# First norm taken for four tiles together, its sums and scalings split between ScalarE and VectorE; x loaded first, the root's table first, first weights in order of use

## The chip, the cores and the metric

One NeuronCore of one Trainium2 chip runs the whole program in one launch. The metric is device time in microseconds (us), as the median of several runs. The engines are named as the profile names them: PE is TensorE (PEld its weight loads), DVE is VectorE, ACT is ScalarE, POOL is GpSimd, SP is SyncE, whose queue issues nearly all DMAs here.

## The reference, cut to what matters

Two transformer blocks follow each other on x of 1024 tokens by 1024 features in float32. The change is in the first lines of the first block:

```python
def rmsnorm(x, w):
    y = x * lax.rsqrt(jnp.mean(x * x, axis=-1, keepdims=True) + EPS)
    return y * w

mem_n = rmsnorm(mem, norm_mem_w)                      # mem: 256 x 1024
proj = rmsnorm(h, norm_mix_w) @ w_in                  # h = x
ca, cb, rq, rk, rv, rg = jnp.split(proj, cuts, axis=-1)
u = ca * jax.nn.sigmoid(cb)                           # 512 channels each
y = depthwise_conv_31(u) + conv_b                     # causal, 31 taps
```

Behind them come a retention over rq, rk, rv and rg, a cross attention to mem_n, a feed-forward layer, and the second block with windowed attention and 16 experts. None of these is edited.

## The kernel before, in words

x is handled as eight tiles of 128 rows (tokens) by 1024 features, in two halves of four tiles, and mem as two such tiles. For each tile `unit_rows` sums the squares on ACT (`sumsq`, L182), takes the root of the mean (`rsqrt_of`, L164 to L175: one small instruction on ACT, L166, and six on DVE) and scales the tile on DVE (L189). `to_fm` then transposes the four tiles of a half on PE (L222, each 128x128 block by itself into `ptT`), and writes for each of the eight feature blocks a pair `hT`: a rounded high part on ACT (L204), and on DVE the rest (L205). Every product is made of three matmuls (L139, L140, L141) from such pairs. A weight unit of 512 KB is loaded as `raw` (three buffers) and split into a pair `w` (five buffers) by ACT (L114) and DVE (L115).

The first products are `cb` and `ca`, 24 matmuls each for a block of 128 channels and a half of the tokens; `sg` is the sigmoid of `cb` (L381) and `uh` the product with `ca` (L385). Each `u` goes to DRAM and comes back for the convolution, 31 DVE instructions for each of four channel blocks (L393, L395). Their result `y` also goes to DRAM and comes back as `yh`, which PE transposes into `yc` (L565). The convolution stands in the program with a low priority, so that its instructions fill DVE beside the next products (`qk`, `v`, `rg`), and beside the retention, which goes through eight tiles in turn (`qkT`, `qbd`, `sc`, `pf`, `yin`, `yT`, `kv`). `km` is the key product of the cross attention; it does not depend on the retention, and stands between its matmuls.

Each engine and the SP queue work strictly in their own order. A scheduler sets that order from priorities and from its own estimates; `tc.high_priority(offset=...)` moves what is written under it ahead by so many places.

Of the kernel before, what the change touches and what calls it, by code (L numbers as in the profile page):

```python
# [12 lines left out]
BF = mybir.dt.bfloat16  # L13
I32 = mybir.dt.int32
U32 = mybir.dt.uint32
AF = mybir.ActivationFunctionType
OP = mybir.AluOpType
# [4 lines left out]
D = 1024  # L22
# [12 lines left out]
def tile_kernel(ctx: ExitStack, tc: tile.TileContext, d, out, stop=None, dbg=None):  # L35
    nc = tc.nc
    pe, act, dve, pool = nc.tensor, nc.scalar, nc.vector, nc.gpsimd
# [21 lines left out]
    def R(i, shape, dt=F32, name="r"):  # L59
        return sb.tile(shape, dt, tag=f"R{i}", bufs=1, name=nm(name))  # L60
# [22 lines left out]


    ident = cst.tile([128, 128], F32, name="ident")
    with tc.high_priority(offset=4500):
        nc.sync.dma_start(ident, d["ident"])
    small = cst.tile([128, 216], F32, name="small")
    with tc.high_priority(offset=4000):
        nc.sync.dma_start(small, d["small"])  # L90
    kc = cst.tile([128, 40], F32, name="kc")
    nc.sync.dma_start(kc, d["kconst"])
# [33 lines left out]
    def wunits(src, i0, n, ahead=1500):  # L126

        res = []
        with tc.high_priority(offset=ahead):
            for u in range(i0, i0 + n):  # L130
                raw = raw_unit(src[u])
                w = sb.tile([128, 2, 1024], F32R, tag=f"W{w_ring[0]()}", bufs=1, name=nm("w"))
                split(w[:, 0, :], w[:, 1, :], raw)
                res.append(w)
        return res
# [52 lines left out]
    def unit_rows(x):  # L188
        dve.tensor_scalar(x, x, row_rstd(x), None, op0=OP.mult)  # L189
        return x  # L190

    def scaled(dst, x, r, gain):
        dve.scalar_tensor_tensor(dst, x, r, gain, op0=OP.mult, op1=OP.mult)
# [22 lines left out]
    def to_fm(xs, regs, banks, name="hT", gain=None, shift=None):  # L216

        res = []
        for k, reg in enumerate(regs):
            p = B(banks(), "ptT")  # L220
            for j, x in enumerate(xs):
                pe.transpose(p[:, j * 128:(j + 1) * 128], x[:, k * 128:(k + 1) * 128], ident)  # L222
            h = R(reg, [128, 2, 512], F32R, name=name)
            evac_split(h[:, 0, :], h[:, 1, :], p, col(gain, k), col(shift, k))
            res.append(h)
        return res
# [66 lines left out]
    def rows(t, n=1):  # L293
        return slice(t * 128, (t + n) * 128)
# [5 lines left out]
    def load(t, src):  # L300
        nc.sync.dma_start(t, src)
        return t
# [13 lines left out]
    pm = Ring([0, 1, 2, 3, 4])  # L316
    pt = Ring([5, 6, 7])
    hT = {}
    for half in range(2):
        with tc.high_priority(offset=4000 if half == 0 else 0):  # L320
            xs = [load(R([17, 18, 19, 20, 24, 25, 26, 27][half * 4 + j], [128, 1024], name="x"), x_d[rows(half * 4 + j), :])
                  for j in range(4)]
            hT[half] = to_fm([unit_rows(x) for x in xs], H[half], pt, gain=g_in)

    xs = [unit_rows(load(R(28 + j, [128, 1024], name="mem"), d["mem"][rows(j), :])) for j in range(2)]
    memT = fm_pairs(xs, [16, 22, 23, 32], pt, g_mem)


# [43 lines left out]
    tr = Ring([0, 1])  # L372
    tr2 = Ring([2, 3])
    for c in range(4):
        ua, ub = wunits(d["w_in_fm"], 2 * c, 2)
        for half in range(2):
            sl = slice(half * HALF, (half + 1) * HALF)
            p = B(pm(), "cb")
            fm_block(p, ub, half_of(hT, half))
            sg = T(tr(), [128, 512], name="sg")  # L380
            act.activation(sg, p, AF.Sigmoid)  # L381
            p = B(pm(), "ca")
            fm_block(p, ua, half_of(hT, half))
            uh = T(tr2(), [128, 512], name="uh")
            dve.tensor_mul(uh, p, sg)  # L385
            store(u_d[c][:, sl], uh)
# [422 lines left out]
    for t in range(8):  # L809
        x = acc[t]  # L810
# [480 lines left out]
def layout(inputs):  # L1291
    f = {k: np.asarray(v) for k, v in inputs.items()}
    a = dict(_constants())
    a["x"] = f["x"][0]
    a["positions"] = np.ascontiguousarray(f["positions"].reshape(8, 128).T)
    small = np.zeros((128, 216), np.float32)
    small[:, 0:124] = np.transpose(f["conv_w"].reshape(31, 4, 128), (2, 1, 0)).reshape(128, 124)
    small[:, 124:128] = _colp(f["conv_b"])
    small[:, 128:140] = np.transpose(f["conv_w_2"].reshape(3, 4, 128), (2, 1, 0)).reshape(128, 12)
    for i, n in enumerate(("norm_mix_w", "norm_xattn_w", "norm_mlp_w", "norm_mem_w")):  # L1300
        small[:, 156 + 8 * i:164 + 8 * i] = _colp(f[n])
    small[:, 188:196] = _colp(f["g_mix_2"][0])
    small[:, 196:204] = _colp(f["g_ffn_2"][0])
    for i, n in enumerate(("ret_gn_w", "conv_ln_w", "conv_ln_b")):
        small[:, 204 + 4 * i:208 + 4 * i] = _colp(f[n])
    a["small"] = small
    a["norm_f_w"] = f["norm_f_w"]
    a["g_ffn"] = f["g_ffn_2"][0]
    a["g_final"] = f["g_final_2"]
    a["sink"] = f["sink_2"][0]  # L1310
    a["mem"] = f["mem"][0]
    a["ctx"] = f["ctx_2"][0]
    bcol = _colp(f["b_ada_2"][0])
    a["b_col"] = np.ascontiguousarray(np.concatenate([bcol, bcol[:, :16]], 1))
    a["c_rows"] = np.stack([f["c_2"][0], f["c_ctx_2"]])
    W = f["w_in"]
    a["w_in_fm"] = _fm(W, [x for c in range(4) for x in (c * 128, 512 + c * 128)])
    a["w_in_tm"] = _tm(W, [2048, 1024, 1536])
    a["w_out_tm"] = _tm(f["w_out"], [0, 512])
    a["xk_fm"] = _fm(f["xkv_w"], range(0, 1024, 128))  # L1320
    a["xv_tm"] = _tm(f["xkv_w"], [1024, 1536])
    a["xq_fm"] = _fm(f["xq_w"], range(0, 1024, 128))
    a["xo_tm"] = _tm(f["xo_w"], [0, 512])
    a["up_fm"] = _fm(f["mlp_up_w"], range(0, 4096, 128))
    dn = f["mlp_down_w"]
    chunks, r0 = [], 0
    for fbs in MLP_CHUNKS:
        chunks.append(_tm(dn[r0:r0 + fbs * 128], [0, 512]))
        r0 += fbs * 128
    a["down_tm"] = np.concatenate(chunks, 0)  # L1330
    a["w_ada"] = np.ascontiguousarray(f["w_ada_2"][0].T.reshape(48, 128, 1024))
    W = f["w_in_2"][0]
    a["w_in2_q"] = _tm(W, [0])
    b = W[:, 512:768].reshape(2, 4, 128, 256)
    a["w_in2_kv"] = np.ascontiguousarray(np.transpose(b, (0, 2, 1, 3)).reshape(2, 128, 1024))
    a["w_in2_fm"] = _fm(W, [x for c in range(4) for x in (1280 + c * 128, 1792 + c * 128, 768 + c * 128)])
    a["w_out2_tm"] = _tm(f["w_out_2"][0], [0, 512])
    a["w_router"] = np.ascontiguousarray(np.transpose(f["w_router_2"][0].reshape(8, 128, 16), (1, 0, 2)).reshape(128, 128))
    wg, wu, wd = f["w_gate_2"][0], f["w_up_2"][0], f["w_down_2"][0]
    ex = []  # L1340
    for e in range(16):
        for nb in (0, 512):
            ex += [_tm(wg[e], [nb]), _tm(wu[e], [nb])]
        for kp in (0, 512):
            ex += [_tm(wd[e][kp:kp + 512], [0, 512])]
    a["experts"] = np.concatenate(ex, 0)
    return a
# [19 lines left out]
```

## Time and profile before

| | |
|---|---|
| median of 3 runs | 2571.12 us (2568.53 to 2572.6) |
| the profiled execution | 2569.4 us, its span 2567.6 us |
| PE busy | 2433.2 us, 95% of the span |
| DVE busy | 1792.5 us, 70% |
| ACT busy | 1164.9 us, 45% |
| granted TensorE clock, mean | 0.98 |

The span is the time from the first to the last instruction; the rest of the execution's own time lies around it. Busy shares are means over stages that differ: in some PE is the only full engine, in some DVE is full too.

### The profile page before, as it was taken

What the parts mean: (1) busy time and instruction counts of PE and PEld (TensorE: products, weight loads), DVE (VectorE), ACT (ScalarE), POOL (GpSimd) and SP (SyncE); (2) the same over time, 40 slices, a digit from 0 to 9 for tenths busy, and PEclk for the clock granted to TensorE, in tenths of its full rate; (3) what the DMA queues carried; (4) which work ended last, traced back from release to release, by engine and by line L of the source; (5) the groups of instructions that cost most, each with busy time, mean ns of one, the idle gap of its engine ahead of it and who ended that gap; (6) DMA issues with size and microseconds to landing.
All of it is one profiled execution on the core that took longest, in us unless ns stands there. A gap on an engine that the chain in (4) does not pass through costs nothing.

```text
span 2567.6 us, 31478 instructions
## 1 busy us (share of the span) xinstructions
PE 2433.2 (95%) x11473; PEld 1971.9 (77%) x11473; DVE 1792.5 (70%) x3204; ACT 1164.9 (45%) x1783; POOL 54.5 (2%) x35
## 2 busy tenths in 40 slices
PE   7999899999999999999999999998973999999996
PEld 5887678888878888888888777776863888888774
DVE  6999783655577555333336858876567999999888
ACT  6113552544442122112214635554332888887775
POOL 0000000000000000000000000000000110101100
PEclk9999999999999999999999999999986999999998
DMA  5233545425443344211112221125673999999993
GB/s 192 87 122 119 161 160 193 142 97 164 137 155 123 119 144 156 64 42 48 58 50 78 92 74 50 42 62 171 219 272 112 384 397 390 390 391 385 354 349 148
DMA packets 138476, 442.34 MB, mean 172 GB/s; under 512 B 15664, under 2 KB 20304, under 8 KB 138320
## 3 DMA queue, kind: packets, MB, share of 16 engines
q1 hardware_dynamic: 133856, 424.07, 46.4%
q0 software_dynamic: 4464, 16.25, 2.6%
q8 instruction: 90, 1.47, 0.2%
q14 instruction: 66, 0.54, 0.1%
HBM read 388.34 MB, written 51.92 MB: 171 GB/s over the span
## 4 chain that ended last, share of the span: by engine, by line
PE 82%; DVE 8%; DMA 5%; ACT 3%; issue 2%; SPq 0%; ACTq 0%; DVEq 0%; POOLq 0%
PE up L140 7%; PE up L141 7%; PE up L139 7%; PE dn L140 6%; PE dn L141 6%; PE dn L139 6%; PE wo L139 3%; PE wo L140 3%; PE wo L141 3%; PE ga L140 2%; PE ga L141 2%; PE ga L139 2%; DVE w L115 2%; PE q L140 2%; PE q L141 2%
## 5 line engine op out<-in xcount | busy, mean ns | idle before, releaser
L114 ACT ACTIVATE w<-raw 128x1024 fp32r<-128x1024 f32 x560 | 584.3, 1059 | 752.1 <-PE dn L141 266.4
L115 DVE TENSOR_TENSOR w<-raw,w 128x1024 fp32r<-128x1024 f32 x560 | 673.5, 1222 | 187.7 <-ACT w L114 180.8
L139 PE MATMUL dn<-w,uT 128*128 128x512 f32 x512 | 199.4, 390 | 1.8 <-ACT relu L754 1.6
L139 PE MATMUL up<-hm,w 128*128 128x512 f32 x512 | 199.6, 390 | 0.0
L140 PE MATMUL up<-hm,w 128*128 128x512 f32 x512 | 199.4, 389 | 0.0
L141 PE MATMUL up<-hm,w 128*128 128x512 f32 x512 | 199.3, 389 | 0.0
L140 PE MATMUL dn<-w,uT 128*128 128x512 f32 x512 | 199.0, 389 | 0.0
L141 PE MATMUL dn<-w,uT 128*128 128x512 f32 x512 | 198.6, 389 | 0.0
L773 DVE TENSOR_TENSOR acc<-dn,acc 128x512 f32<-128x512 f32 x144 | 97.9, 687 | 91.8 <-PE dn L141 91.4
L738 DVE CUSTOM_DVE_ANT_0 mws<-wada,crow 128x512 bf16<-128x512 f32 x128 | 88.2, 689 | 103.0 <-DMA wada<-w_ada 101.0
L395 DVE SCALAR_TENSOR_TENSOR y<-u,small,y 128x1007 f32<-128x1007 f32 (+26 forms) x120 | 146.2, 1260 | 0.5
L139 PEld LDWEIGHTS dn<-w,uT 128*128 128x128 f32 x512 | 96.1, 188 | 22.9 <-ACT relu L754 2.3
L141 PEld LDWEIGHTS up<-hm,w 128*128 128x128 f32 x512 | 96.1, 188 | 20.0
L141 PEld LDWEIGHTS dn<-w,uT 128*128 128x128 f32 x512 | 96.0, 188 | 20.1 <-DVE uT L759 0.2
L139 PEld LDWEIGHTS up<-hm,w 128*128 128x128 f32 x512 | 96.0, 188 | 20.0 <-ACT hm L204 0.3
L140 PEld LDWEIGHTS dn<-w,uT 128*128 128x128 f32 x512 | 96.1, 188 | 19.8
L140 PEld LDWEIGHTS up<-hm,w 128*128 128x128 f32 x512 | 96.1, 188 | 19.8
L140 PE MATMUL ga<-w,x1T 128*128 128x512 f32 x256 | 102.5, 400 | 1.7 <-DVE w L115 1.7
L140 PE MATMUL dn<-w,x1T 128*128 128x512 f32 x256 | 101.6, 397 | 2.0 <-DVE w L115 2.0
L139 PE MATMUL dn<-w,x1T 128*128 128x512 f32 x256 | 102.3, 400 | 0.0
L141 PE MATMUL ga<-w,x1T 128*128 128x512 f32 x256 | 102.0, 398 | 0.0
L140 PE MATMUL up<-w,x1T 128*128 128x512 f32 x256 | 101.6, 397 | 0.0
(414 smaller groups left out, 5471.2 us busy)
## 6 DMA issues: line engine op xcount, KB each, us to landing
raw<-experts SPq DMA_DIRECT2D x384, 512.0 KB, 7.2
wada<-w_ada SPq DMA_DIRECT2D x48, 512.0 KB, 3.5
raw<-up_fm SPq DMA_DIRECT2D x32, 512.0 KB, 3.6
raw<-down_tm SPq DMA_DIRECT2D x32, 512.0 KB, 3.6
raw<-w_out_tm SPq DMA_DIRECT2D x24, 512.0 KB, 3.9
raw<-w_in_fm SPq DMA_DIRECT2D x20, 512.0 KB, 3.8
h_d<-hx SPq DMA_DIRECT2D x32, 256.0 KB, 2.4
raw<-xq_fm SPq DMA_DIRECT2D x16, 512.0 KB, 4.3
```

Of the source, the lines that this page charges most:

```text
L114: act.activation(hi, src, AF.Copy)
L115: dve.tensor_sub(lo, src, hi.bitcast(F32))
L139: pe.matmul(out_, l[0], r[0], start=first, stop=False)
L140: pe.matmul(out_, l[0], r[1], start=False, stop=False)
L141: pe.matmul(out_, l[1], r[0], start=False, stop=last)
L395: dve.scalar_tensor_tensor(yc[:, s:], uc[:, :1024 - s], convw[:, c, 30 - s:31 - s], yc[:, s:], op0=OP.mult, op1=OP.add)
L738: dve.tensor_tensor_reduce(out=mjunk, in0=raw[:, h * 512:(h + 1) * 512], in1=crow[o, h], op0=OP.mult, op1=OP.add, scale=1.0, scalar=0.0, a ...
L773: dve.tensor_add(acc[t][:, sl], p, acc[t][:, sl])
```

## The change

`unit_tiles` takes a list of tiles. It puts the sums of squares of its tiles into the columns of one small tile, those of even tiles on ACT, those of odd tiles on DVE (a new instruction, `tensor_tensor_reduce`); it takes the roots of all columns at once; then it scales even tiles on DVE and odd ones on ACT. It is used for both halves of x and for the two tiles of mem. The loads of the constants `ident` and `small` now stand behind those of x, a root of a constant at the start brings the root's table to ACT, and of each pair of weight units the one for `cb` now comes first.

```diff
-    with tc.high_priority(offset=4500):
+    with tc.high_priority(offset=3900):
         nc.sync.dma_start(ident, d["ident"])
     small = cst.tile([128, 216], F32, name="small")
-    with tc.high_priority(offset=4000):
+    with tc.high_priority(offset=3890):
         nc.sync.dma_start(small, d["small"])
...
+    junk2 = T(6, [128, 1024], BF, name="junk2")
+
+    def unit_tiles(xs):
+
+        n = len(xs)
+        ss = tiny([128, n])
+        for j, x in enumerate(xs):
+            if j % 2 == 0:
+                act.activation(junk, x, AF.Square, accum_out=ss[:, j:j + 1])
+            else:
+                dve.tensor_tensor_reduce(out=junk2, in0=x, in1=x, op0=OP.mult, op1=OP.add, scale=1.0, scalar=0.0,
+                                         accum_out=ss[:, j:j + 1])
+        r = rsqrt_of(ss, 1.0 / D, n)
+        for j, x in enumerate(xs):
+            if j % 2 == 0:
+                dve.tensor_scalar(x, x, r[:, j:j + 1], None, op0=OP.mult)
+            else:
+                act.activation(x, x, AF.Copy, scale=r[:, j:j + 1])
+        return xs
...
+    warm = tiny([128, 1])
+    with tc.high_priority(offset=4500):
+        dve.memset(warm, 1.0)
+        act.activation(warm, warm, AF.Sqrt)
...
-            hT[half] = to_fm([unit_rows(x) for x in xs], H[half], pt, gain=g_in)
-
-    xs = [unit_rows(load(R(28 + j, [128, 1024], name="mem"), d["mem"][rows(j), :])) for j in range(2)]
+            hT[half] = to_fm(unit_tiles(xs), H[half], pt, gain=g_in)
+
+    xs = unit_tiles([load(R(28 + j, [128, 1024], name="mem"), d["mem"][rows(j), :]) for j in range(2)])
...
-        ua, ub = wunits(d["w_in_fm"], 2 * c, 2)
+        ub, ua = wunits(d["w_in_fm"], 2 * c, 2)
...
-    a["w_in_fm"] = _fm(W, [x for c in range(4) for x in (c * 128, 512 + c * 128)])
+    a["w_in_fm"] = _fm(W, [x for c in range(4) for x in (512 + c * 128, c * 128)])
```

The lines behind the edits move by 20 to 24 (L204 becomes L224, L565 becomes L589). The scheduler's order changes in two stretches: in the first 320 matmuls, and again where the retention, `km` and `yc` are mixed. Behind that PE's order is the same as before.

ACT at the program's start, before (`x_73` to `x_79` are the four tiles of the first half):

```order
L182 ACT_TABLE_LOAD
L182 ACTIVATE junk,y_81<-x_73 128x1024
L182 ACTIVATE junk,y_96<-x_75 128x1024
L166 ACT_TABLE_LOAD
L166 ACTIVATE y_85<-y_83 128x1
L182 ACTIVATE junk,y_111<-x_77 128x1024
L166 ACTIVATE y_100<-y_98 128x1
L182 ACTIVATE junk,y_126<-x_79 128x1024
L166 ACTIVATE y_115<-y_113 128x1
L166 ACTIVATE y_130<-y_128 128x1
L114 ACTIVATE w_447<-raw_445 128x1024
L114 ACTIVATE w_452<-raw_450 128x1024
```

The same place now (`x_77` to `x_83` are the four tiles; their even ones are summed here, their odd ones scaled):

```order
L342 ACT_TABLE_LOAD
L342 ACTIVATE y_74<-y_74 128x1
L200 ACTIVATE junk,y_85<-x_77 128x1024
L200 ACTIVATE junk,y_85<-x_81 128x1024
L166 ACTIVATE y_92<-y_90 128x4
L209 ACTIVATE x_79<-x_79,y_100 128x1024
L209 ACTIVATE x_83<-x_83,y_100 128x1024
L114 ACTIVATE w_360<-raw_358 128x1024
L224 ACTIVATE hT_111<-ptT_106,small 128x512
L224 ACTIVATE hT_119<-ptT_114,small 128x512
L224 ACTIVATE hT_127<-ptT_122,small 128x512
```

Four sums, four roots and a table load became two sums, one root and two scalings; one weight split stands between them and the first `hT`, where before there were three.

ACT where the second half is normed, before (`x_205` to `x_211` are its tiles):

```order
L166 ACTIVATE y_217<-y_215 128x1
L182 ACTIVATE junk,y_228<-x_207 128x1024
L381 ACT_TABLE_LOAD
L381 ACTIVATE sg_480<-cb_455 128x512
L166 ACT_TABLE_LOAD
L166 ACTIVATE y_232<-y_230 128x1
L182 ACTIVATE junk,y_243<-x_209 128x1024
L166 ACTIVATE y_247<-y_245 128x1
L182 ACTIVATE junk,y_258<-x_211 128x1024
```

And now (`x_170` to `x_176`; `cb_488` is the second channel block's product, `ws` the angles of the rotary embedding):

```order
L200 ACTIVATE junk,y_267<-mem_263 128x1024
L405 ACTIVATE sg_513<-cb_488 128x512
L166 ACT_TABLE_LOAD
L166 ACTIVATE y_272<-y_270 128x2
L166 ACTIVATE y_185<-y_183 128x4
L209 ACTIVATE mem_265<-mem_265,y_280 128x1024
L209 ACTIVATE x_172<-x_172,y_193 128x1024
L209 ACTIVATE x_176<-x_176,y_193 128x1024
L391 ACT_TABLE_LOAD
L391 ACTIVATE ws_328<-ws_328 128x128
L224 ACTIVATE hT_204<-ptT_199,small 128x512
```

The root of the second half now stands behind a sigmoid that reads the second channel block's product, and its first `hT` behind a table load and a sine. On SP the last tile, `x_176`, is issued behind three weight loads, the last of which waits for the split of the fifth unit; before, the last tile stood behind two.

PE in the retention's fourth tile, before (`kv`, `sc`, `yin`, `yx` are the retention, `km` the filler):

```order
L141 MATMUL km_2944<-hP_406,w_2941 128x256
L453 MATMUL qkT_2127<-ident,qr_2123 128x128 x4
L462 MATMUL sc_2137<-qbd_1396,qkT_1755 128x512
L499 MATMUL kv_2046<-vl_2001,kz_2044 128x256 x2
L462 MATMUL sc_2141<-qbd_1396,qkT_1755 128x512
L471 MATMUL yin_2146<-pf_2139,vl_2125 128x256 x2
L484 MATMUL yx_2162<-St_1395,qkT_1755 128x256
L565 MATMUL yc_2626<-ident,yh_2621 128x128
L565 MATMUL yc_2649<-ident,yh_2621 128x128
```

And now:

```order
L141 MATMUL km_2981<-hP_289,w_2973 128x256
L139 MATMUL km_2981<-hP_299,w_2973 128x256
L523 MATMUL kv_1959<-vl_1914,kz_1957 128x256 x2
L486 MATMUL sc_2050<-qbd_1309,qkT_1668 128x512
L486 MATMUL sc_2054<-qbd_1309,qkT_1668 128x512
L495 MATMUL yin_2059<-pf_2052,vl_2038 128x256 x2
L508 MATMUL yx_2075<-St_1308,qkT_1668 128x256
L589 MATMUL yc_2539<-ident,yh_2534 128x128
L589 MATMUL yc_2562<-ident,yh_2534 128x128
```

`kv` now stands ahead of both `sc`, and seven more `km` ahead of it. Before, the first two `yc` that read the third and fourth channel block stood 22 `km` ahead of this place, among those of the first head; now they stand behind the whole of it.

## Rows read from the trace of the kernel before

**Rows 1.** The page's chain that ended last: shares of the span by engine.

```profile
PE 82%; DVE 8%; DMA 5%; ACT 3%; issue 2%; SPq 0%; ACTq 0%; DVEq 0%; POOLq 0%
```

**Rows 2.** Windows: stretch, its length, busy us of each engine, granted clock, DMA.

```profile
core 0: us, PE busy (x) PEld busy (x) DVE busy (x) ACT busy (x) POOL busy (x), PEclk, DMA share, GB/s
0.00:19.00 19.00, 3.67 (x13) 2.07 (x13) 9.11 (x32) 11.22 (x19) 0.20 (x4) 1.00 0.76 269
5.00:10.00 5.00, 0.00 (x0) 0.00 (x0) 0.52 (x4) 4.06 (x7) 0.00 (x0) 1.00 1.01 411
52.00:225.00 173.00, 173.00 (x764) 143.28 (x764) 164.61 (x166) 30.97 (x39) 0.00 (x0) 1.00 0.33 110
272.00:285.00 13.00, 7.60 (x35) 6.12 (x34) 5.82 (x23) 6.06 (x10) 0.00 (x0) 0.75 0.58 189
285.00:300.50 15.50, 15.24 (x79) 11.98 (x79) 10.86 (x43) 8.48 (x18) 0.00 (x0) 0.88 0.30 92
400.00:2567.00 2167.00, 2062.86 (x9735) 1676.85 (x9733) 1446.70 (x2485) 1003.24 (x1497) 54.30 (x31) 0.98 0.51 178
```

**Rows 3.** Timeline of the first half: start, duration, engine, instruction, [idle before <-releaser].

```profile
1.64 1.85 SPq L301 DMA_DIRECT2D x<-x  x4
5.52 1.06 ACT L182 ACTIVATE junk<-x 128x1024 bf16<-128x1024 f32 x1 [3.50 <-DMA x<-x]
7.06 1.06 ACT L182 ACTIVATE junk<-x 128x1024 bf16<-128x1024 f32 x1 [0.40 <-DMA x<-x]
8.23 1.28 ACT L166 ACT_TABLE_LOAD   x1
9.76 0.16 DVE L168 RECIPROCAL y<-y 128x1 f32<-128x1 f32 x1 [1.36 <-ACT y L166]
10.73 0.75 DVE L189 TENSOR_SCALAR x<-x,y 128x1024 f32<-128x1024 f32 x1
16.89 0.74 DVE L189 TENSOR_SCALAR x<-x,y 128x1024 f32<-128x1024 f32 x1
18.20 1.84 ACT L204 ACTIVATE hT<-ptT,small 128x512 fp32r<-128x512 f32 x3 [2.74 <-PE ptT L222]
18.94 0.80 PE L139 MATMUL cb<-hT,w 128*128 128x512 f32 x1 [0.35 <-ACT hT L204]
28.42 0.39 PE L141 MATMUL cb<-hT,w 128*128 128x512 f32 x1
```

**Rows 4.** Instruction groups by form, 0 to 60 us: count, busy us, mean ns, idle before.

```profile
L205 DVE SCALAR_TENSOR_TENSOR hT<-ptT,small,hT 128x512 fp32r<-128x512 f32 x16 | 11.6, 745 | 1.6 <-ACT hT L204 1.6
L115 DVE TENSOR_TENSOR w<-raw,w 128x1024 fp32r<-128x1024 f32 x7 | 8.6, 1222 | 1.0 <-ACT w L114 1.0
```

**Rows 5.** The page's costliest groups: the only DVE instruction with a sum.

```profile
L738 DVE CUSTOM_DVE_ANT_0 mws<-wada,crow 128x512 bf16<-128x512 f32 x128 | 88.2, 689 | 103.0 <-DMA wada<-w_ada 101.0
```

**Rows 6.** Timeline of the second half's norm and of the first product.

```profile
29.12 0.43 SPq L301 DMA_DIRECT2D x<-x  x1
35.30 1.06 ACT L182 ACTIVATE junk<-x 128x1024 bf16<-128x1024 f32 x1 [1.25 <-DMA x<-x]
39.69 0.74 DVE L189 TENSOR_SCALAR x<-x,y 128x1024 f32<-128x1024 f32 x1
40.84 1.84 ACT L204 ACTIVATE hT<-ptT,small 128x512 fp32r<-128x512 f32 x3 [1.27 <-PE ptT L222]
52.07 0.39 PE L140 MATMUL ca<-hT,w 128*128 128x512 f32 x1
57.58 0.69 DVE L385 TENSOR_TENSOR uh<-ca,sg 128x512 f32<-128x512 f32 x1 [2.07 <-PE ca L141]
```

**Rows 7.** Timeline: start of the convolution, and PE's two longest waits behind it.

```profile
64.68 0.82 DVE L393 TENSOR_SCALAR y<-u,small 128x1024 f32<-128x1024 f32 x1 [0.76 <-DMA u<-u]
274.53 0.44 PE L565 MATMUL yc<-ident,yh 128*128 128x128 f32 x2 [2.09 <-DMA yh<-y]
282.85 2.07 PE L462 MATMUL sc<-qbd,qkT 128*128 128x512 f32 x2 [3.31 <-ACT qbd L458]
```

## The prediction

> **What bounds the kernel now.** The chain that ended last comes first: 82% of it is PE [rows 1]. The windows then show where PE is not full [rows 2]. Until 19 us it is busy for 3.7 us, so over 15 us pass before the first product. From 52 to 225 us it never stops: 764 matmuls in 173 us, 0.226 us each. From 400 us on it is busy for 2062.9 of 2167 us. Those later stages are not edited and their order does not move, so a lead that PE has at 400 us should stand at the end. The place to look for a loss on the way is DVE, which is busy for 164.6 of the same 173 us: the convolution fills it from 64.68 on [rows 7]. From 272 to 285 us both engines have holes, PE 5.4 us and DVE 7.2 us, and PE's granted clock is 0.75 there [rows 2]; its two long waits are named in [rows 7]. So three places decide: the start, the second half's norm near 40 us, and the stretch from 272 us.
>
> **First half.** Four issues of x take 1.85 us, so two fewer ahead of x bring it 0.9 us forward: the first sum, which waits for its tile until 5.52, starts at 4.6. The second tile came 1.54 us behind the first [rows 3]; at the 411 GB/s of that stretch [rows 2] a tile of 0.52 MB takes 1.28. With 1.4, the four land at 4.6, 6.0, 7.4 and 8.8. ACT sums the first and third beside the landing. The last sum is DVE's, an instruction that this trace lacks. Its nearest row sums 512 columns from two sources in 0.69 us [rows 5], and a two-source DVE pass over 1024 takes 1.22 [rows 4]; with reading the sum out I take 1.3. The lower bound is ACT's 1.06 [rows 3], the upper one twice the pass, 2.4. So the sums stand at 10.1. The mean and the root add 0.4, the reciprocal and its polish 0.97 (from 9.76 to 10.73), so scaling starts at 11.5. DVE's two scalings (0.75 each) lie beside ACT's two, 1.06 each: ACT ends at 13.55. Before, the last tile's scaling ended at 16.89 + 0.74 = 17.63. What goes: the second table load (1.28, at 8.23) and a root behind each sum on ACT.
>
> Then ACT's order puts a weight split (a pass over 1024, 1.06) ahead of the first `hT`, which lasts 0.69: PE's first `cb` starts at 15.25, where it started at 18.94, 3.7 us earlier. The eight rests of `hT` on DVE (0.745 each) pace the block, with three weight splits (1.22) between them: 9.6 us, less about 0.1 for each that follows closely. From 14.55 the last rest ends at 23.5, and the block's last matmul some 0.6 later, at 24.1, where it ended at 28.8. After the first half PE leads by about 4.5 us. That the `cb` unit now comes first costs nothing and gives nothing of its own: before, both units were split while ACT waited for transposes until 18.20 [rows 3]. With the slow sum all of this comes 1.1 us later.
>
> **Second half.** PE then has `ca` and the second channel block's `cb` and `ca`, 71 matmuls of 0.226, until 40.2. The second half's root stands behind the sigmoid of that `cb`, which ends 47 matmuls on, at 34.75. Then come the sigmoid 0.6, a table load 1.28 and two roots: 37.0. On DVE some 18 small instructions of 0.16 (the two norms' and those of the angles between them) lead to the first scaling at 39.9. ACT scales a tile of mem, then two of x: the last ends at 41.6, then a sine's table (1.28), the sine and the first `hT`: 43.9. PE has 12 transposes in the meantime and waits for about 2.4 us. Before, that `hT` was written at 40.84 [rows 6], 2.4 us sooner than now, but PE had done 24 matmuls fewer. The rest of this interleaving is DVE's again, an estimate of 7.6 us: eight rests 0.7 apart, and 2 us for three parts of mem and for transposes that wait for a free bank: PE is dense from 51.5 with 16 matmuls more behind it than before at 52.07. The lead is 0.6 + 16 x 0.226 = **4.2 us**.
>
> SP now issues the last x tile behind three weight loads, the last of which waits for two more splits on DVE, at about 27. Before, it was issued at 29.12 and landed by 35.30 [rows 6]. If it takes as long it lands at 33.2; its sum and the memory tile's then end at 35.8, and the means are ready ahead of the root's 36.8. Each us beyond 34.2 would cost one. Ten norms of six small DVE instructions became three (42 fewer, 6.7 us), five scalings left DVE (3.7) and five sums came (6.5); the net 4 us are free, all of it ahead of 45 us, where DVE waits anyway.
>
> **The convolution and the stretch from 272 us.** Here is what speaks against the change. The first `uh` needs both halves of the first channel block. PE now does the second channel block's first half before that, so this `ca` ends 34 matmuls after 51.5, and `uh` starts at 59.4 where it started at 57.58 [rows 6]. The convolution starts 1.8 us later while PE leads by 4.2, so by any point behind it DVE still has 6.0 us of convolution to do, five of its instructions. The order keeps PE's needs ahead of them, so PE keeps its lead to 272 us. Then DVE must do the 6.0 us in its own holes: 7.2 us until 285 and 4.6 more until 300.5 [rows 2]. I reckon DVE packed until the fourth tile's `pf` (284.96 before), which turns 7.2 - 6.0 = 1.2 us of holes into lead, and no gain behind that. `yc`, whose wait of 2.09 us began this slack, stands further back, behind 29 more `km`; `kv` now waits for DVE's `kz` ahead of `sc`, so PE's hole stays, only filled by DVE. Bounds: none of the holes can be used, and the 4.2 us are lost; or all 11.8 us until 300.5 can, which gives 5.8.
>
> **Sum.** 4.2 + 1.2 = 5.4 us, from the profiled execution's 2569.4 to 2564.0. That execution lies 1.7 us under the median of 2571.1, so the forecast for the median is **2565.7 us**, its own range 2563 to 2568.
>
> **Rivals.**
> The clock falls while PE waits near 42 us. For it: behind the waits of 2.09 and 3.31 us the granted clock is 0.75 until 285 and 0.88 until 300.5 [rows 2, 7], and the new wait of 2.4 us lies between those two. Against it: until 19 us PE is nearly idle and the view still gives 1.00, though its `cb` of 18.94 lasts 0.80 where that of 28.42 lasts 0.39 [rows 3]. At half of 2.4 GHz, 0.88 over 15.5 us is 3.7 us at the lower level, 0.75 over 13 us is 6.5 us; five us at that level cost 2.5. The lead falls to 1.7 and the total to 2568.2. The Trainium skill, page "TensorE: Matmul & The Clock Gate", section "Part 1: The HAM clock gate", has the throttled clock as the resting state, which steady work lifts and idleness brings back. By that rule the new wait is a danger, and the trace agrees at 272 us.
>
> DVE can't place the convolution's rest, since retention waits for what stands behind it in DVE's order: the lead is gone at 300 us, 2571. For it is the 95% of DVE's 173 us, against it the 7.2 us of holes.
>
> All holes go: 4.2 + 5.8 = 10.0 us, 2561.1. For it is that PE's clock loss there would go too; against it, the new order of `kv`.
>
> Slower: the convolution's tail. Its last instruction now stands behind two weight splits and the third tile's `yt`, which I put near 278, and `y` still goes to DRAM and back. `yc` stands in PE's order ahead of the rest of the fourth tile, so PE waits if `yh` is late. With two transfers of some 4 to 5 us (from issue to landing, half to all of the 6.2 us above) it lands at 286 to 288, when PE is near there. Landing at 291 takes the whole lead; from 296 on the kernel is slower by more than 5 us, say 2577.
>
> **Chances and range.** A measurement of this kernel can't tell changes under about 0.2%, 5.1 us. Forecast 0.42, all holes 0.22, clock 0.18, no lead left 0.10, slower 0.08. The forecast's own range lies half on either side of 2566.0, so faster is 0.21 + 0.23 = 0.44, same 0.21 + 0.27 = 0.48, slower 0.08. The range leaves out the slower case, and takes in the bounds of the new sum and of the holes: 2559 to 2571.5.
>
> **What would show it.** A first `cb` near 15.3, the first block's last near 24; no ACT table load between the sums and the root; the second half's first `hT` near 44 behind a PE wait of 2 to 3 us, with granted clock 1.00; `uh` near 59.4 and the convolution near 66.5; PE dense to 225 and some 4 us ahead at each landmark; the fourth tile's `sc` near 277 and DVE without holes before it. The prediction is wrong if the last x lands after 35, if the clock falls near 45, if `yc` waits for more than 2 us, or if the lead changes behind 400 us.

## The result, and the profile after

The changed kernel takes 2591.16 us (median of 4 runs, 2587.63 to 2595.72); the kernel before, run beside it, took 2569.82 us (4 runs). The ratio is 1.0086, with a 95% interval of 1.0072 to 1.0099: **slower by 21 us by the medians, 22 by the ratio**, where 5.4 us of gain were forecast. The profiled execution is the one of 2587.63 us. The chain that ended last, of the changed kernel, is PE as before [rows 1]:

```profile
PE 83%; DVE 8%; DMA 4%; ACT 3%; issue 2%; SPq 0%; ACTq 0%; DVEq 0%; POOLq 0%
```

The start went nearly as forecast. The timeline of the first half, of the changed kernel (start, duration, engine, instruction, [idle before <-releaser]; compare [rows 3]):

```profile
0.73 1.28 ACT L342 ACT_TABLE_LOAD   x1 [0.73 <-PEq L1376]
4.34 1.06 ACT L200 ACTIVATE junk<-x 128x1024 bf16<-128x1024 f32 x1 [2.11 <-DMA x<-x]
9.24 1.22 DVE L202 CUSTOM_DVE_ANT_0 junk<-x 128x1024 bf16<-128x1024 f32 x1 [2.41 <-DMA x<-x]
10.39 0.08 DVE L202 DVE_READ_ACCUMULATOR2_ANT y<- 128x1 f32 x1
12.02 2.19 ACT L209 ACTIVATE x<-x,y 128x1024 f32<-128x1024 f32 x2 [1.04 <-DVE y L175]
15.79 0.80 PE L139 MATMUL cb<-hT,w 128*128 128x512 f32 x1
19.61 0.77 PE L139 MATMUL cb<-hT,w 128*128 128x512 f32 x1
```

The first `cb` starts at 15.79, 3.15 us earlier than before. The windows of the changed kernel, the same stretches as in [rows 2]:

```profile
core 0: us, PE busy (x) PEld busy (x) DVE busy (x) ACT busy (x) POOL busy (x), PEclk, DMA share, GB/s
52.00:225.00 173.00, 173.00 (x755) 140.20 (x753) 159.35 (x165) 32.93 (x44) 0.00 (x0) 1.00 0.32 107
272.00:285.00 13.00, 8.89 (x65) 7.80 (x63) 12.76 (x38) 6.21 (x12) 0.00 (x0) 0.95 0.57 186
285.00:300.50 15.50, 15.12 (x84) 12.22 (x85) 11.61 (x43) 9.68 (x20) 0.00 (x0) 0.93 0.54 172
400.00:2585.00 2185.00, 2082.79 (x9741) 1678.21 (x9739) 1448.25 (x2485) 1003.34 (x1497) 54.37 (x31) 0.98 0.50 177
```

From 272 to 285 us DVE is now packed, and PE's clock is 0.95 where it was 0.75. But look at the first line. PE is busy for all of the 173 us, at full clock, as before, and does 755 matmuls where it did 764. No wait can be seen, since there is none: each matmul takes longer. From 400 us to the end PE is busy for 19.9 us more (2082.79 against 2062.86) with the same matmuls but for six. The clearest stretch is 800 to 1400 us, where the program's order is that of before and PE does nothing but `up` and `dn`. Its window, of the kernel before and then of the changed one:

```profile
800.00:1400.00 600.00, 600.00 (x2649) 496.82 (x2648) 269.48 (x527) 136.42 (x192) 0.00 (x0) 1.00 0.27 86
```

```profile
800.00:1400.00 600.00, 600.00 (x2613) 490.82 (x2613) 263.79 (x497) 129.27 (x178) 0.00 (x0) 1.00 0.27 85
```

That is 600/2649 = 0.2265 us and 600/2613 = 0.2296 us from one matmul to the next. The groups by form of that stretch, of the changed kernel, show which are slower (mean ns of one, to an end that is modelled):

```profile
L139 PE MATMUL up<-hm,w 128*128 128x512 f32 x448 | 176.7, 394 | 0.0
L140 PE MATMUL up<-hm,w 128*128 128x512 f32 x448 | 176.1, 393 | 0.0
L140 PE MATMUL dn<-w,uT 128*128 128x512 f32 x423 | 165.6, 391 | 0.0
```

Before, every group of that stretch had 389:

```profile
L139 PE MATMUL up<-hm,w 128*128 128x512 f32 x448 | 174.3, 389 | 0.0
```

How far ahead of the kernel before PE stands at its n-th matmul, from the two traces (start times, n counted from 0):

| n | 200 | 900 | 1,200 | 1,500 | 3,500 | 6,000 | 8,500 | last |
|---|---|---|---|---|---|---|---|---|
| before, us | 57.54 | 216.20 | 291.57 | 349.52 | 769.27 | 1335.94 | 1840.41 | 2546.27 |
| lead of the changed kernel | 0.65 | -3.04 | 0.22 | -1.35 | -3.66 | -11.29 | -15.98 | -18.19 |

The lead falls wherever PE is dense, and some of it came back between the 1,000th matmul (-3.37) and the 1,500th, where DVE's holes were filled. (From the 1,100th to the 1,200th the count gives 4.6 us, but there the order differs, so the two kernels' n-th matmuls are not the same instruction.) What edits of the first 45 us have to do with a matmul at 1000 us is not to be seen in any row, since the profile shows no addresses. It is in the program's allocation: an address in a partition for each tile name, given out in the order in which names come up. Small tiles take 32 bytes each. Before, the first norms brought up 24 of them (768 bytes) ahead of the first half's hT and 8 (256 bytes) between the two halves' hT. Now one stands ahead of x, and 6 (192 bytes) at each of three places. So the large tiles on either side moved against each other: `w` less hT was 150848 - 37952 = 441 x 256 bytes for the first half and 150848 - 87360 = 248 x 256 for the second; now it is 152480 - 39456, which leaves 128 over a multiple of 256, and 152480 - 88800, which leaves 192.

### The profile page after: what moved, and what is told of

It reads as the page before. It is cut to its first block, busy times and chain, and to the rows that moved or that the text cites. A ratio compares the mean times of both kernels' runs of the same rounds, so it can differ in the third digit from the quotient of the medians.

```text
span 2585.8 us, 31429 instructions
## 1 busy us (share of the span) xinstructions
PE 2455.4 (95%) x11473; PEld 1972.7 (76%) x11473; DVE 1791.4 (69%) x3168; ACT 1163.5 (45%) x1771; POOL 54.6 (2%) x35
## 4 chain that ended last, share of the span: by engine, by line
PE 83%; DVE 8%; DMA 4%; ACT 3%; issue 2%; SPq 0%; ACTq 0%; DVEq 0%; POOLq 0%
PE up L140 7%; PE up L141 7%; PE up L139 7%; PE dn L140 6%; PE dn L139 6%; PE dn L141 6%; PE wo L140 3%; PE wo L139 3%; PE wo L141 3%; PE ga L140 2%; PE ga L141 2%; PE ga L139 2%; PE q L141 2%; PE q L140 2%; PE q L139 2%
## 5 line engine op out<-in xcount | busy, mean ns | idle before, releaser
L139 PE MATMUL up<-hm,w 128*128 128x512 f32 x512 | 202.2, 395 | 0.0
L141 PE MATMUL up<-hm,w 128*128 128x512 f32 x512 | 201.7, 394 | 0.0
L140 PE MATMUL up<-hm,w 128*128 128x512 f32 x512 | 201.4, 393 | 0.0
L419 DVE SCALAR_TENSOR_TENSOR y<-u,small,y 128x1023 f32<-128x1023 f32 (+25 forms) x120 | 146.0, 1263 | 0.4
```

The costliest lines, as they stand in the source:

```text
L139: pe.matmul(out_, l[0], r[0], start=first, stop=False)
L140: pe.matmul(out_, l[0], r[1], start=False, stop=False)
L141: pe.matmul(out_, l[1], r[0], start=False, stop=last)
L419: dve.scalar_tensor_tensor(yc[:, s:], uc[:, :1024 - s], convw[:, c, 30 - s:31 - s], yc[:, s:], op0=OP.mult, op1=OP.add)
```

## The experiments

**e1, e2, e3, e4: shifts.** The first theory was that operands off a multiple of 64 bytes are slow, since 10,109 of the changed kernel's matmuls stream one and none of before does. The rival was the new order. The first edit is that of e1 (on the changed kernel) and of e2 (on the kernel before); e3 has 232 columns in place of 224, on the kernel before. Each makes a constant tile that lies ahead of the others 32 (e3: 64) bytes wider, and so moves everything behind it together.

```diff
-    small = cst.tile([128, 216], F32, name="small")
+    small = cst.tile([128, 224], F32, name="small")
...
-        nc.sync.dma_start(small, d["small"])
+        nc.sync.dma_start(small[:, :216], d["small"])
```

And that of e4, on the kernel before, which moves the weights against the rest:

```diff
-        raw = sb.tile([128, 1024], F32, tag=f"{pre}{i}", bufs=1, name=nm("raw"))
+        raw = sb.tile([128, 1032 if (pre, i) == ("raw", 0) else 1024], F32, tag=f"{pre}{i}", bufs=1, name=nm("raw"))[:, :1024]
```

> The changed kernel with the constant tile `small` made 224 columns wide instead of 216 (the added 32 bytes a partition are never read): every tile allocated behind it lies 32 bytes higher, and nothing else is different. By the allocation, all 11,324 matmuls of the kernel before stream their moving operand from an address that is a multiple of 64 bytes; in the changed kernel 10,109 of them start 32 bytes off such a multiple, and with this edit none does. Theory A (addresses): the loss comes from these offsets; matmuls in the dense stretches are back at 0.226 us each (884 in 200 us at 800 to 1400, where the changed kernel had 872), and the time is what the front's lead gives, 2563 to 2567 us. Theory B (order: the scheduler's new order makes engines meet differently at the memory): the order is that of the changed kernel, so the matmuls stay at 0.229 us and the time at 2588 to 2596 us.

Measured: 2590.21 us, ratio to the kernel before 1.0078 (1.0061 to 1.0095), 2613 matmuls in 800 to 1400. Nothing came back.

> The kernel before with the same 32 bytes added to `small`: now 10,109 of 11,324 moving operands start 32 bytes off a multiple of 64, in the old order. Theory A: matmuls at 800 to 1400 take 0.229 us (about 872 in 200 us), and the time rises by the 22 us that the changed kernel lost and the 4 to 5 us that its front gained, to 2592 to 2598 us. Theory B: 0.226 us and 2568 to 2572 us, as the kernel before.

Measured: 2567.87 us, 0.9995 (0.9986 to 1.0005), 2649 matmuls. With 10,109 operands 32 bytes off, nothing was lost: **theory A has fallen.**

> The kernel before with 64 bytes added to `small`: every tile lies elsewhere than before, but the moving operands start at multiples of 64 again. Theory A: 2568 to 2572 us. Theory C (any shift does it, because tiles now share some larger block of memory with others): a slower time, 2580 us or more, as in the other shift of the kernel before.

Measured: 2567.85 us, 0.9997 (0.9987 to 1.0006). A shift of everything costs nothing.

> The kernel before with only the first `raw` buffer made 32 bytes larger: the weight pairs `w` and what is allocated behind them move by 32 bytes, the pairs hT, hm and nearly all uT stay. `qk`, `v`, `rg` and `dn` now stream `w` from 32 bytes off (6,453 moving operands in all), while `cb`, `ca` and `up` hold `w` as weights and stream hT or hm from multiples of 64 as before. Theory A1 (the streamed operand counts): qk, v and dn slower than 0.227 us, ca, cb and up at 0.227 us, the time 2578 to 2588 us. Theory A2 (the loaded weights count): ca, cb and up slower, qk, v and dn at 0.227 us. Theory B: all at 0.227 us and 2568 to 2572 us.

Measured: 2604.88 us, 1.0135 (1.0118 to 1.0152): 36 us lost in the old order, and neither A1 nor A2, since all are slow. The groups by form of 800 to 1400 us, of e4:

```profile
L139 PE MATMUL up<-hm,w 128*128 128x512 f32 x448 | 177.2, 395 | 0.0
L139 PE MATMUL dn<-w,uT 128*128 128x512 f32 x411 | 162.0, 394 | 0.0
```

Theory B, for which the kernel before must not change when its tiles move, can't explain e4. What e1 left as it was and e4 changed is the distance between the two operands of a matmul. Sorted by it (the gap: address of the streamed operand less that of the weights, modulo 256), the traces of these runs fall into line, whatever the tile, kernel or order: about 0.227 us from start to start at gap 0, 0.229 at 64, 0.2325 at 128 and 0.233 at 192, 224 and 32. This is theory D, made from these traces; the next runs try it.

**e5, e6, e7: gaps set on purpose.** The edit of e5 (on the changed kernel) and of e6 (on the kernel before); e7 is the edit of e4 with 1040 in place of 1032, on the kernel before.

```diff
     sb = ctx.enter_context(tc.tile_pool(name="sb", bufs=1))
+    yp = ctx.enter_context(tc.tile_pool(name="yp", bufs=1))
...
-        return sb.tile(shape, F32, tag=f"y{role or ''}{n % ring}", bufs=1, name=nm("y"))
+        return yp.tile(shape, F32, tag=f"y{role or ''}{n % ring}", bufs=1, name=nm("y"))
```

> The changed kernel with its small tiles in a pool of their own, so that they no longer lie between the large tiles; nothing else is different. Call gap the address at which a matmul's streamed operand starts minus the address of its weights, modulo 256 bytes. In the kernel before 9,112 of the 9,960 fp32r matmuls have gap 0, in the changed kernel 2,060 (2,752 have 128, 2,316 have 64, 1,984 have 192, 848 have 32); with this edit all have 0. Theory D (the gap sets PE's pace; read from the earlier traces as 0.227 us at 0, 0.229 at 64, 0.2325 at 128, 0.233 at 192, 224 and 32): outside the experts the changed kernel pays about 2,752 x 5.4 + 2,316 x 2.2 + 1,170 x 6.3 ns = 27 us for its gaps, so this kernel takes 2560 to 2566 us and has 884 matmuls in 200 us at 800 to 1400. Theory B (the new order does it): 2588 to 2596 us and 872 matmuls.

Measured: 2565.76 us, ratio to the kernel before 0.9983 (0.9974 to 0.9991), 25.4 us under the changed kernel, where the sum over its gaps gave 27. The small tiles now get their addresses in a region of their own (a pool), and no longer lie between the large ones. The window of e5, 2648 matmuls at the old pace:

```profile
800.00:1400.00 600.00, 600.00 (x2648) 496.75 (x2647) 269.35 (x524) 135.79 (x192) 0.00 (x0) 1.00 0.27 86
```

> The kernel before with its small tiles in a pool of their own: all 9,960 gaps are 0, where 848 were 192, most of them in the experts. Theory D: there DVE is busy 95% of the time, so of the 848 x 6.3 ns = 5 us between nothing and all shows, 2563 to 2570 us; the pace at 800 to 1400 stays (884). Theory B: 2568 to 2572 us. What the front's part of the change is worth is the difference between this run and the changed kernel with its own pool: the forecast's lead says 5 us.

Measured: 2566.26 us, 0.9989 (0.9980 to 0.9998). The difference of e6 to e5 is 0.5 us, not 5, and not clear of noise: with the addresses cured, the change gives almost nothing. That is the second question, taken up in e9 to e11.

> The kernel before with the first `raw` buffer 64 bytes larger: in the old order 5,244 matmuls get gap 64 and 3,896 get 192, and every operand still starts at a multiple of 64. Theory D: outside the experts about 3,700 x 2.2 + 3,100 x 6.3 ns = 28 us more, 2592 to 2600 us; qk, v and dn (gap 64) at 0.229 us, ca, cb and up (gap 192) at 0.233. Theory B, and theory A kept for the 32-byte shift alone (only an operand off a multiple of 64 is slow): 2568 to 2572 us.

Measured: 2592.19 us, 1.0084 (1.0065 to 1.0104), at the lower end of theory D's range, and 2595 matmuls in 800 to 1400. Every operand starts at a multiple of 64 here and nothing of the order is new. By gap, from start to start: 0.2293 us at 64 (`dn`) and 0.233 at 192 (`up`).

**e8: PE alone.** The core of the program:

```diff
+    for gap in [0] + gaps + gaps[::-1]:
+        o = 2048 + gap // 4
+        for g in range(12):
+            p = B(pm(), f"gap{gap}b")
+            for k in range(8):
+                pe.matmul(p, big[:, k * 128:(k + 1) * 128], big[:, o:o + 512], start=k == 0, stop=k == 7)
```

> Matmuls alone: the whole computation is left out; the program loads four tiles of x, rounds them to fp32r, runs 19 groups of 96 fp32r matmuls 128x128 by 128x512 whose streamed operand lies 0, 32, 64, 96, 128, 160, 192, 224 and 256 bytes beyond a multiple of 256 from the weights, in this order and back (with one group at 0 ahead), and stores a constant tile as output. No other engine and no DMA works beside the matmuls. Theory D: 0.227 us a matmul at 0 and 256, 0.229 at 64, 0.2325 at 128, 0.233 at 32, 192 and 224, the same in both passes. Theory E (the gap matters only by what the other engines and DMAs do at the memory meanwhile): the same pace in all groups.

The timeline of e8, first pass and the turn (start, length of the whole group, its 96 matmuls):

```profile
55.53 22.57 PE L328 MATMUL gap32b<-big 128*128 128x512 f32 x96
77.93 22.15 PE L328 MATMUL gap64b<-big 128*128 128x512 f32 x96
99.92 22.57 PE L328 MATMUL gap96b<-big 128*128 128x512 f32 x96
122.33 22.56 PE L328 MATMUL gap128b<-big 128*128 128x512 f32 x96
144.72 22.65 PE L328 MATMUL gap160b<-big 128*128 128x512 f32 x96
167.21 22.55 PE L328 MATMUL gap192b<-big 128*128 128x512 f32 x96
189.60 22.55 PE L328 MATMUL gap224b<-big 128*128 128x512 f32 x96
211.99 43.69 PE L328 MATMUL gap256b<-big 128*128 128x512 f32 x192
255.51 22.56 PE L328 MATMUL gap224b<-big 128*128 128x512 f32 x96
```

From the start of a group to that of the next, per matmul: (77.93 - 55.53)/96 = 0.2333 us at gap 32, then 0.2291 (64), 0.2334 (96), 0.2332 (128), 0.2343 (160), 0.2332 (192), 0.2332 (224), and (255.51 - 211.99)/192 = 0.2267 at 256. The way back repeats these, within 0.001 us. It is a single execution; in it no other engine was busy beside the matmuls and the DMAs moved 0 to 1 GB/s, so theory E has fallen: the gap sets the pace without the others.

**e12: which weights?** The same with other weights, `o` being 2048 and `g` a quarter of the gap:

```diff
+                pe.matmul(p, big[:, k * 128:(k + 1) * 128], big[:, o:o + 512], start=k == 0, stop=False)
+                pe.matmul(p, big[:, (k + 1) * 128:(k + 2) * 128], big[:, o:o + 512], start=False, stop=False)
+                pe.matmul(p, big[:, (k + 2) * 128 - g:(k + 3) * 128 - g], big[:, o:o + 512], start=False, stop=False)
+                pe.matmul(p, big[:, (k + 3) * 128 - g:(k + 4) * 128 - g], big[:, o:o + 512], start=False, stop=k == 4)
```

> Matmuls alone again (the computation is left out in the same way as in the run e8, and a constant tile is stored): now the weights alternate, two matmuls with gap 0 and two with gap g, so that on four lines stand the four pairs of a matmul's own gap and the gap of the next one, whose weights load while it streams: own 0 and next 0, own 0 and next g, own g and next g, own g and next 0; with g of 128, 64, 32, 16 and 128 again, 12 groups of 8 each. Theory D1 (the weights that load meanwhile are what the streamed operand meets): the time from one start to the next is 0.227 us where the next gap is 0, and for g = 128 0.233 where it is g, whatever the matmul's own gap is. Theory D2 (the weights already held count): it follows the own gap. A gap of 16 was not in any earlier run.

From start to start, in the order of the four lines: 0.2267, 0.2266, 0.2267 and 0.2267 us for g of 16; 0.2314, 0.2307, 0.2315 and 0.2300 for 32; 0.2302, 0.2318, 0.2308 and 0.2318 for 64; 0.2305, 0.2305, 0.2355 and 0.2338 for 128 (its second pass, at full clock). Neither D1 nor D2: all four pairs are slow together, and with g of 64 slower than where all gaps were 64 (0.2291). Only at 128 are the two with an own gap of 128 the slower ones (0.2355 and 0.2338 against 0.2305), as D2 would have it, but the other two don't come back to 0.227. A gap of 16 costs nothing. **Which weights the streamed operand meets stays open.**

**e9, e10, e11: where did the front's gain go?** The timeline of e5, where the second half comes in:

```profile
34.76 1.22 DVE L203 CUSTOM_DVE_ANT_0 junk<-x 128x1024 bf16<-128x1024 f32 x1 [4.23 <-DMA x<-x]
42.80 2.58 PE L243 MATMUL ptT<-ident,x 128*128 128x128 f32 x12 [2.19 <-DVE x L208]
46.42 0.80 PE L140 MATMUL cb<-hT,w 128*128 128x512 f32 x1 [1.05 <-ACT hT L225]
```

The last tile lands near 34.7, its sum is read out at 36, and yet the scalings come only at 42; the transposes of all four tiles stand in one lump behind them. The window of e5 there shows the clock gone too:

```profile
42.00:48.00 6.00, 4.15 (x16) 3.38 (x17) 4.47 (x11) 5.69 (x9) 0.00 (x0) 0.59 0.12 45
```

The edit of e9 (on e5), and of e11 (on e6):

```diff
-        with tc.high_priority(offset=4000 if half == 0 else 0):
+        with tc.high_priority(offset=4000 if half == 0 else 1000):
```

And that of e10, on e5:

```diff
-            hT[half] = to_fm(unit_tiles(xs), H[half], pt, gain=g_in)
+            hT[half] = to_fm(unit_tiles(xs) if half == 0 else [unit_rows(x) for x in xs], H[half], pt, gain=g_in)
...
-    xs = unit_tiles([load(R(28 + j, [128, 1024], name="mem"), d["mem"][rows(j), :]) for j in range(2)])
+    xs = ([unit_rows(x) for x in [load(R(28 + j, [128, 1024], name="mem"), d["mem"][rows(j), :]) for j in range(2)]])
```

> The changed kernel with its small tiles in a pool of their own (all gaps 0, as the run e5), and the second half's loads, norm and transposes written under a priority of 1000 where there was none: its x tiles are now issued ahead of the fifth weight unit, and its root and scalings stand before the second sigmoid and the angles. In the profiled execution of the run e5 PE was 5.8 us ahead at its 100th matmul of the kernel before with the same pool, then waited for the second half (7.40 us idle between 34 and 47 us counting its start, with the clock at half speed from 43.1 to 49.9 us), and was 1.9 us ahead at the 200th. Theory F (the front's lead holds to the end if the second half does not hold PE up): no wait of PE over 1 us before 60 us, a lead of 5 to 6 us at the 200th matmul, and an end 4 to 6 us earlier than the kernel before with its own pool, 2560 to 2562.5 us. Theory G (a lead at 60 us is given back between 225 and 400 us, where PE waits for the convolution and the retention): the lead is there at the 200th matmul and under 2 us at the 1,700th, and the time is 2564 to 2566 us.

Measured: 2567.64 us, 1.0000 (0.9991 to 1.0009), above the range of theory F and of theory G. PE's longest wait between 20 and 60 us was 1.32 us.

> The changed kernel with its own pool for small tiles, in which only the first half is normed jointly; the second half and mem are normed tile by tile as before. If the joint root of the second half is what made PE wait for it (each scaling then waits for the last sum), PE's wait between 34 and 48 us shrinks from 5 to under 2 us and the time is 2562 to 2564 us; if it is the late landing of the second half's last tile (34.7 us) and the angles between DVE's steps, the wait stays and the time is 2565 to 2567 us.

Measured: **2561.97 us, 0.9973 (0.9964 to 0.9982)**, the fastest of all, at the fast end of the first answer's range, and 4.3 us under e6. Against the kernel before, run beside each, the difference of e10 and e6 is 0.0016, or 4.1 us, and the two intervals hardly touch. The window of e10 at the same place, PE without a wait, full, and its clock 1.00:

```profile
42.00:48.00 6.00, 6.00 (x36) 4.83 (x35) 5.67 (x16) 4.87 (x8) 0.00 (x0) 1.00 0.00 0
```

> The kernel before with its own pool for small tiles and the priority of 1000 for the second half, without the change itself: what that edit alone is worth. PE waited there 1 to 2 us for the second half, so theory F says 2564 to 2566 us, and theory G no difference from 2566 us; the difference of the run e9 to this one is what the joint norm is worth when it isn't followed by a wait (4 to 5 us by theory F, under 2 us by theory G).

Measured: 2570.16 us, 1.0002 (0.9993 to 1.0011); theory G's 2566 is missed too, by 4 us to the worse. e9 lies 2.5 us under it, between what F and G said, and the intervals overlap.

PE's lead over e6 at its n-th matmul, in the profiled executions:

| n | 100 | 200 | 1,000 | 1,500 | 1,600 | 4,500 | last |
|---|---|---|---|---|---|---|---|
| e6, us | 39.91 | 59.97 | 241.52 | 348.98 | 370.42 | 995.60 | 2545.63 |
| e5, all normed jointly | 5.82 | 1.94 | 1.94 | 0.58 | 0.61 | -0.84 | 0.26 |
| e9, second half ahead | 6.53 | 6.49 | 6.34 | 9.22 | 0.52 | 1.33 | 3.47 |
| e10, first half jointly | 3.97 | 5.26 | 4.93 | 3.95 | 3.95 | 4.52 | 4.64 |

By this table theory F would hold for e10: what PE has at the 200th matmul stands, with little change, at the end. But single traces are too weak for that. e2 and e3, which norm as e6 does, are 3.51 and 3.75 us ahead of e6 at the 200th matmul and 4.54 and 4.06 at the last, so the trace of e10 ends level with theirs. What e10 is worth rests on the medians.

For e9 theory G seems to hold, at one place: its lead of 9.22 us goes between the 1,500th matmul and the 1,600th. The timeline there, of e9 and then of e11:

```profile
360.66 3.31 PE L603 MATMUL ptz<-ident,z 128*128 128x128 f32 x13 [5.95 <-DVE z L597]
```

```profile
364.15 3.31 PE L579 MATMUL ptz<-ident,z 128*128 128x128 f32 x13 [5.92 <-DVE z L573]
```

PE waits for the convolution's norm, in both. In e6, e5 and e10 its wait for `z` is 0.7 us. e11 has no joint norm, so this wait comes with the priority edit that e9 and e11 share, and not with the joint norm; e9 therefore says little on whether a lead holds. Why `z` came no sooner in e9, though its convolution started at 60.85 and that of e6 at 67.14, was not tried.

Joint or not, then, is not the whole matter; it decides by where the roots stand. In e9 the root is joint too, but ahead, and PE's wait near 42 us is gone. In e10 the roots come tile by tile; three of the four tiles of the second half are scaled by 35.3, and PE transposes them three or four blocks at a time between matmuls, from 30.77 on. The last tile came hardly sooner in e10 (34.25) than in e5 (34.76), so its late landing is not what made PE wait. The timeline of e10:

```profile
30.77 0.52 PE L243 MATMUL ptT<-ident,x 128*128 128x128 f32 x3
34.25 1.06 ACT L183 ACTIVATE junk<-x 128x1024 bf16<-128x1024 f32 x1 [1.87 <-DMA x<-x]
```

## Why the prediction was wrong, point by point

**The step that failed** is "764 matmuls in 173 us, 0.226 us each", taken as given for the kernel after, and with it "a lead that PE has at 400 us should stand at the end". The order behind 400 us did not move, as said, but the tiles did. The term that was missing is the sum over gaps, 27 us by the pace at each gap, 25.4 us by e5 against the changed kernel. Shown: that the distance between operands sets PE's pace (e4 and e7 in the old order, e8 with PE alone), that curing it alone takes the loss away (e5), that the new order doesn't cause it (e5 has that order), and that a common shift neither cures nor causes it (e1 to e3). Not shown: what in PE makes it so. No rival contained it; the forecast's last sentence, that it is wrong "if the lead changes behind 400 us", is what came.

**First half: right, but for PE's own speed.** The new sum, with its reading out, went from 9.24 to 10.47, 1.23 us, where 1.3 was taken from [rows 5] and [rows 4]. Scaling began at 12.02 (11.5 forecast), the first `cb` at 15.79 (15.25). The block's 24th `cb` then started at 26.50, where 24.1 was forecast as its end; in e5 it started at 24.11. The two differ in PE's speed at first: the `cb` of 19.61 in the changed kernel still lasts 0.77 us, while in e5 a `cb` of 17.27 lasts 0.40 (the timeline of e5):

```profile
17.27 0.40 PE L142 MATMUL cb<-hT,w 128*128 128x512 f32 x1
```

How long PE stays slow differs from one execution to the next: in e10, which norms the first half as e5 does, a `cb` of 20.96 still lasts 0.61. The forecast's sum has no term for PE's slow start; it let DVE's rests pace the block.

**Second half: the place right, the size not.** The timeline of ACT in the changed kernel:

```profile
37.84 0.60 ACT L405 ACTIVATE sg<-cb 128x512 f32<-128x512 f32 x1 [7.37 <-PE cb L141]
41.41 1.16 ACT L209 ACTIVATE mem<-mem,y 128x1024 f32<-128x1024 f32 x1 [1.36 <-DVE y L175]
42.47 2.17 ACT L209 ACTIVATE x<-x,y 128x1024 f32<-128x1024 f32 x2
46.17 1.83 ACT L224 ACTIVATE hT<-ptT,small 128x512 fp32r<-128x512 f32 x3
```

The sigmoid came at 37.84 (34.75 forecast) and the first `hT` was written some 0.7 us behind 46.17 (43.9), both 3 us late, as the first block's end was. On the way one term was too small: ACT's three scalings were put 1.7 us behind DVE's first (39.9 to 41.6), but they waited for the same small instructions and ended 3.1 us behind it (41.51 to 44.64). PE waited 1.7 us for that `hT`, where about 2.4 were forecast. The lead at the 200th matmul was 0.65 us, not 4.2. With gap 0 (e5) it was 1.94 over e6, and e9 and e10 show the reason: the place of the joint root. It sends all four tiles through one chain, which here lies behind a sigmoid and between the angles on DVE. The rival "the clock falls while PE waits near 42 us" did not come in the changed kernel's profiled execution, whose clock is 1.00 from 36 to 54 us, but in that of e5: 0.59 from 42 to 48 us, where PE was idle for 1.85 us and transposing for 2.58. The Trainium skill, page "TensorE: Matmul & The Clock Gate", section "Part 1: The HAM clock gate", says that idleness brings the low clock back; this trace agrees. Single profiles of the same order differ there anyway: at the 200th matmul e2 and e3, which norm as e6 does, are 3.5 and 3.8 us ahead of e6, as said above, so the 1.94 us of e5 carry less weight than the medians.

**The convolution and the stretch from 272 us: right in kind, too small.** `uh` started at 63.11 (59.4 forecast, 57.58 before), the convolution at 70.54, so DVE was 5.9 us late. The holes from 272 to 285 us took it up, as reckoned: DVE busy 12.76 of 13 us. That the 6.0 us of the forecast come so near is chance: they were 1.8 us of delay and 4.2 of lead, and here it was nearly all delay. `yc` waited no longer; PE's longest wait there became one of 3.10 us for `yt`. The timeline of the changed kernel:

```profile
63.11 0.69 DVE L409 TENSOR_TENSOR uh<-ca,sg 128x512 f32<-128x512 f32 x1 [3.02 <-PE ca L141]
70.54 0.81 DVE L417 TENSOR_SCALAR y<-u,small 128x1024 f32<-128x1024 f32 x1
282.54 0.63 PE L477 MATMUL qkT<-ident,qr 128*128 128x128 f32 x4 [3.10 <-DVE yt L511]
```

PE won 4.6 us there by the count; from the 1,000th matmul to the 1,500th, between which all of this reordered stretch lies, 2.0 net of the gaps' cost; 1.2 was forecast. Its clock also stayed up (0.95 for 0.75). That need not be the change's doing: the window of e2, in the old order, shows 1.00:

```profile
272.00:285.00 13.00, 9.17 (x53) 7.14 (x53) 9.65 (x38) 7.05 (x16) 0.00 (x0) 1.00 0.59 196
```

The slower rival, a late `yc`, did not come: the 22 us have nothing to do with it.

**The size of the gain.** e10 less e6, -4.3 us by the medians and -4.1 by the ratios, is what the joint first half, the early x and table and the order of weights are worth together where nothing holds PE up after them; no run parts them. The forecast was 5.4: 4.5 us of lead from the first half, 0.3 lost in the second, and 1.2 from DVE's holes. The 0.3 looks too small: e5 less e10 is +3.8 us by the medians and 2.6 by the ratios, but their intervals (0.9974 to 0.9991 and 0.9964 to 0.9982) overlap, so the size of that loss is open.

## What to carry to other kernels

An edit that adds, drops or reshapes a tile, however small, moves the others: compare the addresses of the streamed operand and the weights, modulo 256, before and after, and count matmuls in a stretch whose order did not move. If PE is 100% busy at the same clock and does fewer, no wait will explain it. Small tiles belong in a pool of their own, so that they can't shift the large ones. And where the engine behind a step is busy, do the parts one by one, so that they can be slipped in between (e10 against e5). That a joint step pays where its consumers must wait for all of it anyway, as at the start, is argued: the joint norm of the first half was not run apart from the early loads.

## What the runs showed of the hardware that was not expected

- With operands of 128x128 and 128x512 in fp32r (the type of the pairs), PE takes 0.2267 us a matmul when the two start a multiple of 256 bytes apart in a partition, 0.2291 at 64 bytes over it and 0.233 to 0.234 at 32, 96, 128, 160, 192 and 224, with nothing else running (e8). At 192 it is 2.9% slower, at the same granted clock and with weight loads that last 188 ns either way (mean of both groups).
- 64 and 192 differ (0.2291, 0.2332), so it counts which of the two operands lies further up.
- Where gaps of 0 and 16 alternate, nothing is lost (0.2267); where 0 and 32, 64 or 128 do, all matmuls take 0.230 us or more (e12).
